# Smaller first x pieces kept on chip, a layer norm spread under gate tiles, and later rms statistics in an eight-core encoder block

## Chip, cores and metric

The kernel runs on all 8 cores of one Trainium2 chip. Each core takes half of one of four sequences (2048 tokens and a halo) and needs nothing from the others. The metric is device microseconds of the slowest core. A core has TensorE (PE, matmuls), VectorE (DVE), ScalarE (ACT), GpSimd (POOL), a sync engine (SP) that here only issues transfers, and 16 DMA engines. GpSimd also issues the transfers of the weights, which the program declares f32 in memory and bf16 on the core (the records show each as 128 packets of 2 KB). Matmuls write to PSUM, of which the program rotates six banks, one tile each.

## The reference, cut to what matters

```python
u = rms_norm(h, g_mix)                         # h: 16 meta tokens, then x
z = u @ w_in                                   # [value | gate | pool | gate A | gate B], 1024 each
y_conv = silu(layer_norm(dwconv31(value * sigmoid(gate)))) @ w_conv_out
y_pool = multi_scale_pool(pool) @ w_pool ... @ w_pool_out
h = h + (sigmoid(gateA) * y_conv + sigmoid(gateB) * y_pool) @ w_o
v = rms_norm(h, g_ffn)
h = h + (silu(v @ w_ffn_gate) * (v @ w_ffn_up)) @ w_ffn_down
out = rms_norm(h, g_final)
```

Activations lie with the 1024 channels on partitions (8 blocks of 128, index c or k) and tokens along the row. A "tile" below is one output block of 128 channels by up to 512 tokens, made by 8 accumulating matmuls. The stages on PE are: pool tiles (the head), value/gate tiles with the depthwise convolution, the layer norm with gate tiles A(c,b), B(c,b), pool products P(c,b) and conv products C(c,b) for channel block c and token block b, the output projection, the gate/up tiles of the channel mixer, and the down projection.

## The kernel before

Every operation goes through a small scheduler that derives semaphore waits from the memory touched, in granules of 64 bytes:

```python
GRAN = 64
def gran(self, ap):                  # cut
    lo = (base + o) // GRAN
    hi = (base + o + span - 1) // GRAN + 1
```

The head takes x in five pieces of 416 tokens. Pieces wait for weights on the sync queue:

```python
x_load(0)
for _ in range(2): load_one()        # pool weights 0 and 1
S.wait_prod(POOL, x_sem[0])
prefetch()                           # the other weights, as slots allow (9 slots)
S.wait_prod(SP, slot_sem[3]);  x_load(1)
S.wait_prod(SP, slot_sem[7]);  x_load(2);  x_load(3)
# per piece: squares on ACT, adder tree on DVE, one f32 ones matmul,
# Ln and Exp on ACT, eight scalings of x into uT (bf16) on DVE, eight pool tiles
```

After the convolution come eight f32 statistic matmuls, Ln and Exp, then the folding of two pool weights into one (`weff`), and 32 normalising steps on DVE that are handed out in the background (`pump`). In the output projection the row statistics work like this:

```python
def sumsq(src, n, c, eng, w_=TT):
    a = ac1[n % 2][:, 0:w_]
    if c == 0:
        act(a, src, AF.Square)
    else:
        q = sq1[c % 3][:, 0:w_]              # three scratch tiles in turn
        act(q, src, AF.Square)
        tt(eng, a, a, q, ALU.add)            # on GpSimd here

def rms_stat(n, w_=TT):
    mm(psum[6][:, 0:w_], ones[:], ac1[n % 2][:, 0:w_], True, True)
    t = sq1[0][:, 0:w_]                      # scratch tile 0 again
    act(t, psum[6][:, 0:w_], AF.Ln, bias=e_rms)
    act(psum[7][:, 0:w_], t, AF.Exp, scale=-0.5)

for b in range(NB):
    for c in range(KC):
        ...                                  # 8 matmuls into one of 6 PSUM banks
        tt(DVE, h, ps[:], h, ALU.add)        # residual add, frees the bank
        sumsq(h, b, c, POOL)
        if c == 2 and b > 0:
            rms_stat(b - 1)
            v_norm(b - 1)                    # eight DVE scalings, 5.4 us
```

Of the kernel before, what the change touches and what calls it, by code (L numbers as in the profile page):

```python
# [7 lines left out]
F32 = mybir.dt.float32  # L8
# [5 lines left out]
KC = 8  # L14
# [15 lines left out]
RMS_EPS = 1e-6  # L30
LN_EPS = 1e-5
NSLOT = 9
HW_ = TOK // 2
RW = HW_ + 28
RWP = 1056
# [155 lines left out]
def build_nc():  # L191
# [3 lines left out]
    def din(name, shape, dt=F32):  # L195
        return nc.dram_tensor(name, list(shape), dt, kind="ExternalInput")

    xp_d = din("xp", [NPC, 128, KC * PW])
    xr_d = din("xr", [NB, 128, KC * TT])
    w_in = din("w_in", [40, 128, 1024])  # L200
    w_co = din("w_conv_out", [8, 128, 1024])
# [50 lines left out]

    uT = at("uT", [128, KC, EXT], BF16, oA)
    psb = [at(f"psb{c}", [128, EXT], F32, oB + c * EXT * 4) for c in range(KC)]
    mT = at("mT", [128, KC, TOK], BF16, oM)
    slot = [at(f"wslot{i}", [128, 1024], BF16, oS + i * 2048) for i in range(NSLOT)]
    slotf = [at(f"wslotf{i}", [128, 512], F32, oS + i * 2048) for i in range(NSLOT)]
# [10 lines left out]
    weff = at("weff", [128, KC, 1024], BF16, oW)  # L268


    xoffs = [oM, oM + 13312, oZ, oW]
    xb = [at(f"xb{i}", [128, KC, PW], F32, o) for i, o in enumerate(xoffs)]
    sq0 = [at(f"sq0_{i}", [128, KC, PW], F32, oZ + 13312 * (1 + i)) for i in range(2)]
    lnt = at("lnt", [128, TT], F32, oZ + 13312 * 3)
    assert 13312 * 3 + 2048 <= NZT * 2048


    z = oZ
# [57 lines left out]
    def dsem(name):  # L336
        return Prod(sem(name))

    cst = dsem("d_const")
    slot_sem = [dsem(f"d_slot{i}") for i in range(NSLOT)]  # L340
    x_sem = [dsem(f"d_x{i}") for i in range(4)]
    rep_sem = [dsem(f"d_rep{i}") for i in range(2)]
    ad_sem = [dsem(f"d_ad{i}") for i in range(2)]
    h1_sem = [dsem(f"d_h1{i}") for i in range(3)]
# [38 lines left out]
    for c in range(KC):  # L383
        wl.append((f"val{c}", w_in.ap()[c], False))
        wl.append((f"gate{c}", w_in.ap()[8 + c], False))
    wl.append(("gA0", w_in.ap()[24], False))
    for g in range(4):
        wl.append((f"wpl{g}", w_pl.ap()[g], True))
        wl.append((f"po{2 * g}", w_po.ap()[2 * g], False))
        wl.append((f"po{2 * g + 1}", w_po.ap()[2 * g + 1], False))  # L390
    for c in range(KC):
        if c:
            wl.append((f"gA{c}", w_in.ap()[24 + c], False))
        wl.append((f"gB{c}", w_in.ap()[32 + c], False))
        if c != 0:
            wl.append((f"co{c - 1}", w_co.ap()[c - 1], False))
    wl.append(("co7", w_co.ap()[7], False))
    for c in range(KC):
        wl.append((f"wo{c}", w_o.ap()[c], False))
# [40 lines left out]
            bg.popleft()()  # L440


    for (o, i_) in ((pc[:], pc_d.ap()), (invc[:], ic_d.ap()), (emask[:], em_d.ap())):
        S.dma(SP, cst, o, i_, val=48)
    S.op(DVE, lambda e: e.memset(ones[:], 1.0 / D), [], [ones[:]])
    S.op(DVE, lambda e: e.memset(eps[:, 0:1], RMS_EPS), [], [eps[:, 0:1]])
    S.op(DVE, lambda e: e.memset(eps[:, 1:2], LN_EPS), [], [eps[:, 1:2]])
    e_rms, e_ln = eps[:, 0:1], eps[:, 1:2]
    for r_ in rep:
        S.gran(r_[:])  # L450


    def x_load(p):
        q = p % 4
        S.dma(SP, x_sem[q], xb[q][:].rearrange("p k t -> p (k t)"), xp_d.ap()[p])

    x_load(0)
    for _ in range(2):
        load_one()
    S.wait_prod(POOL, x_sem[0])  # L460
    prefetch()
    S.wait_prod(SP, slot_sem[3])
    x_load(1)
    S.wait_prod(SP, slot_sem[7])
    x_load(2)
    x_load(3)

    def s1_squares(p):
        x = xb[p % 4]
        sq = sq0[p % 2]  # L470
        for h in range(4):
            act(sq[:, 2 * h:2 * h + 2, :], x[:, 2 * h:2 * h + 2, :], AF.Square)
        tt(DVE, sq[:, 0:2, :], sq[:, 0:2, :], sq[:, 2:4, :], ALU.add)
        tt(DVE, sq[:, 4:6, :], sq[:, 4:6, :], sq[:, 6:8, :], ALU.add)
        tt(DVE, sq[:, 0:2, :], sq[:, 0:2, :], sq[:, 4:6, :], ALU.add)
        tt(DVE, sq[:, 0, :], sq[:, 0, :], sq[:, 1, :], ALU.add)

    def s1_rstd(p):
        mm(psum[6][:, 0:PW], ones[:], sq0[p % 2][:, 0, :], True, True)
        act(lnt[:, 0:PW], psum[6][:, 0:PW], AF.Ln, bias=e_rms)  # L480
        act(psum[7][:, 0:PW], lnt[:, 0:PW], AF.Exp, scale=-0.5)

    def s1_scale(p):
        x = xb[p % 4]
        for k in range(KC):
            stt(DVE, uT[:, k, p * PW:(p + 1) * PW], x[:, k, :], pcc(PC_GMIX, k), psum[7][:, 0:PW],
                ALU.mult, ALU.mult)

    def pool_tile(p, c):
        b = nb()  # L490
        for k in range(KC):
            mm(b[:, 0:PW], w(f"pool{c}", k), uT[:, k, p * PW:(p + 1) * PW], k == 0, k == KC - 1)
        act(psb[c][:, p * PW:(p + 1) * PW], b[:, 0:PW], AF.Copy)

    s1_squares(0)
    s1_rstd(0)
    s1_scale(0)
    for p in range(NPC):
        if p + 1 < NPC:
            s1_squares(p + 1)  # L500
        for c in range(KC):
            pool_tile(p, c)
            if c == 2 and p + 1 < NPC:
                s1_rstd(p + 1)
                s1_scale(p + 1)
            if p == NPC - 1:
                release(f"pool{c}")
        if p == 0:
            x_load(4)


    win_done = set()
# [141 lines left out]
    ln_done = set()  # L654

    def C(c, b):
        pump_until(ln_done, b)
        ps = tile_mm(f"co{c}", lambda k: actT[k][b][:])
        i, j = sA.pop((c, b)), t2.pop((c, b))
        tt(DVE, zt[i][:], ps[:], zt[i][:], ALU.mult)  # L660
        tt(DVE, mrg[c][b][:], zt[i][:], zt[j][:], ALU.add)
        zfree.append(i)
        zfree.append(j)
# [9 lines left out]
    pump(len(bg))  # L673

    lnm = {}
    for b in range(NB):
        tok = slice(b * TT, (b + 1) * TT)
        if b == NB - 1:
            pm, pq = psum[6], psum[7]
        else:  # L680
            pm, pq = nb(), nb()
        mm(pm[:], ones[:], acc_s[:, tok], True, True)
        mm(pq[:], ones[:], acc_q[:, tok], True, True)
        i = ztile()
        act(zt[i][:], pm[:], AF.Square)
        if b == NB - 1:
            mean, rstd = pm, psum[7]
            ids = (i,)
        else:
            m_ = ztile()  # L690
            act(zt[m_][:], pm[:], AF.Copy)
            mean, rstd = zt[m_], zt[i]
            ids = (i, m_)
        tt(DVE, zt[i][:], pq[:], zt[i][:], ALU.subtract)
        act(zt[i][:], zt[i][:], AF.Ln, bias=e_ln)
        act(rstd[:], zt[i][:], AF.Exp, scale=-0.5)
        lnm[b] = (mean, rstd, ids)

    def ln_steps(b):
        mean, rstd, ids = lnm[b]  # L700
        out = []
        for c in range(KC):
            def step(c=c):
                d = d_sb[c][b][:]
                tt(DVE, d, d, mean[:], ALU.subtract)
                tt(DVE, d, d, rstd[:], ALU.mult)
            out.append(step)

        def fin():
            for c in range(KC):  # L710
                act(actT[c][b][:], d_sb[c][b][:], AF.Silu, bias=pcc(PC_LNB, c), scale=pcc(PC_LNG, c))
            zfree.extend(ids)
            ln_done.add(b)
        last = out.pop()
        out.append(lambda: (last(), fin()))
        return out

    for b in range(NB):
        bg.extend(ln_steps(b))


    for g in range(4):
        s_ = whome[f"wpl{g}"]
        for km in range(2):
            src = slotf[s_][:, km * 256:(km + 1) * 256]
            ts(DVE, wps[:, g, km, :], src, pcc(PC_PSC, 2 * g + km), ALU.mult)
        for ki in range(2):
            for h in range(2):
                ps = nb()
                for km in range(2):  # L730
                    mm(ps[:], wps[:, g, km, ki * 128:(ki + 1) * 128],
                       w(f"po{2 * g + km}", None, h * 512, (h + 1) * 512), km == 0, km == 1)
                act(weff[:, 2 * g + ki, h * 512:(h + 1) * 512], ps[:], AF.Copy)
            pump(1)
        release(f"wpl{g}", f"po{2 * g}", f"po{2 * g + 1}")
    zfree.extend((0, 1))

    for b in range(NB):
        Bm(0, b)
        pump(1)  # L740
        P(0, b)
        pump(1)
    release("gB0")
    for c in range(1, KC):
        for b in range(NB):
            A(c, b)
            pump(1)
            Bm(c, b)
            pump(1)
            P(c, b)  # L750
            pump(1)
        release(f"gA{c}", f"gB{c}")
        for b in range(NB):
            C(c - 1, b)
        release(f"co{c - 1}")

    def x_res(b):
        q = b % 3
# [32 lines left out]
    for b in range(NB):  # L791
        for c in range(KC):
# [5 lines left out]
            sumsq(h, b, c, POOL)  # L798
            if b == NB - 1:
                release(f"wo{c}")  # L800
            if c == 2 and b > 0:
                rms_stat(b - 1)
                v_norm(b - 1)
                if b == 1:
                    x_res(3)
# [10 lines left out]
        act(s_, pg[:], AF.Silu)  # L816
        tt(DVE, fT[j][:, tok], pu[:], s_, ALU.mult)

    gu(0, 0)
    rms_stat(3)  # L820
    gu(0, 1)
    v_norm(3)
    gu(0, 2)
    for b in range(3):
        gu(1, b)
    gu(0, 3)
# [79 lines left out]
def _host_inputs(inputs):  # L906
# [37 lines left out]
    for core in range(NCORES):  # L944
# [8 lines left out]
        for g, w in enumerate(WINS):  # L953
# [7 lines left out]
                    cnt = min(t + right + 1, T) - max(t - left, 0)  # L961
                invc[:, g * 8 + jj] = 1.0 / cnt
        m = dict(shared)
        m["xp"] = np.ascontiguousarray(
            xe.reshape(NPC, PW, KC, 128).transpose(0, 3, 2, 1)).reshape(NPC, 128, KC * PW)
        m["xr"] = np.ascontiguousarray(
            xe[HALO:HALO + TOK].reshape(NB, TT, KC, 128).transpose(0, 3, 2, 1)).reshape(NB, 128, KC * TT)
        m["invc"] = invc
# [23 lines left out]
```

## Time and profile before

| | before |
|---|---|
| time, median of the runs | 1092.04 us |
| slowest profiled core | 1089.8 us |
| PE busy | 93% of the span |
| 128x512 tile, start to start | 1.73 us |

The page of the profile before: busy time by engine, and the chain of work that ended last, by engine.

```profile
PE 1009.8 (93%) x5628; PEld 485.2 (45%) x5628; DVE 455.7 (42%) x698; ACT 312.3 (29%) x495; POOL 128.8 (12%) x160
PE 84%; DVE 4%; DMA 4%; ACT 3%; issue 3%; POOL 2%; DVEq 0%; SPq 0%; ACTq 0%; POOLq 0%
```

PE is the engine to save time on, but "busy" hides how: a matmul at half clock is busy too. So the waits of PE are read by stretch. First the head (0 to 112 us), then the layer norm (285 to 372), then the output projection (535 to 625). Columns: who waited for whom, us in total, number of waits, longest.

```profile
PE ps L352 <- DVE sq_0_180 L366: 28.3, 3, 23.0
PE ps L352 <- DVE sq_1_181 L366: 9.2, 2, 6.6
PE ps L352 <- DVE uT L373: 2.5, 1, 2.5
...
PE ps L352 <- DVE wps L369: 6.2, 1, 6.2
PE ps L352 <- ACT act_3_128 L363: 4.5, 1, 4.5
PE ps L352 <- DMA wslot_66<-w_pool_out: 1.8, 1, 1.8
...
PE ps L352 <- POOL ac_1_224 L366: 9.1, 2, 5.1
PE ps L352 <- POOL ac_0_223 L366: 1.4, 1, 1.4
```

The first line holds the start: 23.0 of its 28.3 us pass before the first matmul, the rest are waits for squares of later pieces. In the layer norm PE waits for VectorE to get to the fold's input, and at the end for the activations of token block 3. In the projection it waits for GpSimd's sums. Elsewhere the profile shows one wait of PE, 2.0 us for the last row statistics (after 1060 us), which is why only these three places could give much time.

### The profile page before, as it was taken

Reading aid. Unit: us, or ns where it says so; the run is one execution under the profiler, and the core shown is the slowest. Engines: PE = TensorE matmul, PEld = TensorE weight load, DVE = VectorE, ACT = ScalarE, POOL = GpSimd, SP = SyncE. Lnnn points to the kernel's source line nnn. Section 1 sums busy time; section 2 is a strip of 40 time slices with the busy share of each in tenths; the row PEclk is TensorE's granted clock in tenths of the full one; section 3 lists DMA queues with packets and bytes.
Section 4 is the critical chain, followed back from the end, with each engine's and each line's share of the span. In section 5 each row is a group of like instructions: output and inputs, shape, how many; then the busy total and the mean of one; then the engine's idle time right before and its main releaser. Section 6 shows DMA issues by size and latency. Waiting matters only on the chain.

```text
span 1089.8 us, 15507 instructions; the slowest of 8 cores (1081.2 to 1089.8 us)
## 1 busy us (share of the span) xinstructions
PE 1009.8 (93%) x5628; PEld 485.2 (45%) x5628; DVE 455.7 (42%) x698; ACT 312.3 (29%) x495; POOL 128.8 (12%) x160
## 2 busy tenths in 40 slices
PE   0789999999879699999998799999999999999996
PEld 0344555555324244444443344444444444444485
DVE  1453679984358633322346332222112222233454
ACT  2354234333677512222133421111111111121121
POOL 1000212421020000000044501111000000000000
PEclk9899999999979899999999899999999999999998
DMA  7801797766461111111465734544322200603112
GB/s 138 269 1 19 134 184 153 169 146 145 92 104 31 21 29 29 30 29 30 115 233 193 177 56 74 91 89 88 65 39 35 35 1 2 230 1 155 78 78 78
DMA packets 34234, 99.90 MB, mean 92 GB/s; under 512 B 4080, under 2 KB 7280, under 8 KB 31600
## 3 DMA queue, kind: packets, MB, share of 16 engines
q0 software_dynamic: 17024, 35.13, 20.1%
q1 hardware_dynamic: 17136, 63.77, 19.8%
q8 instruction: 47, 0.77, 0.3%
q14 instruction: 27, 0.22, 0.1%
HBM read 111.93 MB, written 21.04 MB: 122 GB/s over the span
## 4 chain that ended last, share of the span: by engine, by line
PE 84%; DVE 4%; DMA 4%; ACT 3%; issue 3%; POOL 2%; DVEq 0%; SPq 0%; ACTq 0%; POOLq 0%
PE ps L352 79%; PE ps L594 5%; DMA xb_176<-xp 1%; DMA xb_177<-xp 1%; POOL ac_1_224 L366 1%; DMA wslot_62<-w_in 1%; DMA wslot_61<-w_pool_out 1%; DVE vT L373 1%; POOL ac_0_223 L366 1%; DVE sq_0_180 L366 0%; DVE sq_1_181 L366 0%; ACT sq_0_180 L363 0%; ACT sq_1_181 L363 0%; ACT L363 0%; ACT sq_0_220 L363 0%
## 5 line engine op out<-in xcount | busy, mean ns | idle before, releaser
L352 PE MATMUL ps<-mT,weff 128*128 128x512 bf16 x256 | 60.5, 379 | 0.0
L352 PE MATMUL ps<-uT,wslot_63 128*128 128x416 bf16 (+1 forms) x216 | 47.7, 365 | 0.0
L352 PE MATMUL ps<-uT,wslot_60 128*128 128x416 bf16 (+1 forms) x216 | 47.7, 365 | 0.0
L352 PE MATMUL ps<-uT,wslot_62 128*128 128x416 bf16 (+1 forms) x184 | 44.4, 390 | 0.0
L363 ACT ACTIVATE sgf_225<-ps 128x512 f32<-128x512 f32 x30 | 17.9, 598 | 82.6 <-PE ps L352 82.6
L363 ACT ACTIVATE sgf_227<-ps 128x512 f32<-128x512 f32 x29 | 17.3, 598 | 81.5 <-PE ps L352 81.5
L363 ACT ACTIVATE sgf_226<-ps 128x512 f32<-128x512 f32 x29 | 17.3, 598 | 80.2 <-PE ps L352 80.2
L352 PE MATMUL ps<-vT,wslot_62 128*128 128x512 bf16 x160 | 39.1, 388 | 0.0
L352 PE MATMUL ps<-uT,wslot_61 128*128 128x416 bf16 (+1 forms) x184 | 38.9, 354 | 0.0
L352 PEld LDWEIGHTS ps<-mT,weff 128*128 128x128 bf16 x256 | 25.1, 98 | 30.4 <-issue 0.3
L352 PE MATMUL ps<-uT,wslot_64 128*128 128x512 bf16 (+1 forms) x176 | 38.3, 363 | 0.0
L352 PE MATMUL ps<-vT,wslot_60 128*128 128x512 bf16 x160 | 37.8, 379 | 0.0
L352 PE MATMUL ps<-vT,wslot_61 128*128 128x512 bf16 x160 | 37.8, 379 | 0.0
L352 PE MATMUL ps<-vT,wslot_63 128*128 128x512 bf16 x160 | 37.8, 379 | 0.0
L352 PE MATMUL ps<-vT,wslot_64 128*128 128x512 bf16 x160 | 37.8, 379 | 0.0
L352 PE MATMUL ps<-vT,wslot_66 128*128 128x512 bf16 x160 | 37.8, 379 | 0.0
L352 PE MATMUL ps<-vT,wslot_67 128*128 128x512 bf16 x160 | 37.8, 379 | 0.0
L352 PE MATMUL ps<-vT,wslot_59 128*128 128x512 bf16 x160 | 37.8, 379 | 0.0
L352 PEld LDWEIGHTS ps<-uT,wslot_63 128*128 128x128 bf16 x216 | 21.6, 101 | 22.9 <-issue 3.4
L352 PEld LDWEIGHTS ps<-uT,wslot_60 128*128 128x128 bf16 x216 | 21.5, 100 | 21.4 <-issue 1.2
L352 PE MATMUL ps<-uT,wslot_66 128*128 128x416 bf16 (+1 forms) x144 | 30.9, 357 | 0.0
L352 PE MATMUL ps<-vT,wslot_65 128*128 128x512 bf16 x128 | 30.2, 379 | 0.0
(1655 smaller groups left out, 1952.4 us busy)
## 6 DMA issues: line engine op xcount, KB each, us to landing
rep_186<-ad SPq DMA_DIRECT2D x32, 263.0 KB, 6.5
rep_187<-ad SPq DMA_DIRECT2D x32, 263.0 KB, 8.0
h1b_217<-xr SPq DMA_DIRECT2D x2, 2048.0 KB, 10.7
h1d<-h1b_217 SPq DMA_DIRECT2D x2, 2048.0 KB, 8.0
h2b_259<-h1d SPq DMA_DIRECT2D x2, 2048.0 KB, 8.5
xb_176<-xp SPq DMA_DIRECT2D x2, 1664.0 KB, 15.1
h1b_218<-xr SPq DMA_DIRECT2D x1, 2048.0 KB, 19.1
h1b_219<-xr SPq DMA_DIRECT2D x1, 2048.0 KB, 11.5
```

What stands on the lines that cost most here:

```text
L352: S.op(PE, lambda e: e.matmul(out, lhsT=lhsT, rhs=rhs, start=start, stop=stop), [lhsT, rhs], [out], signal=stop if signal is None else signal)
L363: S.op(ACT, lambda e: e.activation(out=out, in_=in_, func=func, scale=scale, **kw), reads, [out])
L366: S.op(eng, lambda e: e.tensor_tensor(out=out, in0=a, in1=b, op=op), [a, b], [out])
L373: S.op(eng, lambda e: e.scalar_tensor_tensor(out=out, in0=a, scalar=s, in1=b, op0=op0, op1=op1), [a, b] + ([] if isinstance(s, float) else ...
L594: S.op(PE, lambda e, o=o, lt=lt, r_=r_, q=q, j=j: e.matmul(o, lhsT=lt, rhs=r_, start=(q == 0), stop=(q == 7), tile_position=(0, 32 * j)), ...
```

## The change

It has three parts. The head gets pieces of 160, 320 and four times 400 tokens that all have a place of their own, with piece 0's statistics summed on PE instead of in an adder tree. The layer norm's statistics go between A(1) tiles, the folds between B tiles, and the silu just ahead of its use. The rms statistics of the output projection move from tile 2 to tile 6 of the next block, and the last one behind three gate/up tiles.

```diff
+PIECES = ((0, 160), (160, 320), (480, 400), (880, 400), (1280, 400), (1680, 400))
...
+    x_load(0)
     for (o, i_) in ((pc[:], pc_d.ap()), (invc[:], ic_d.ap()), (emask[:], em_d.ap())):
         S.dma(SP, cst, o, i_, val=48)
+    for p in range(1, NX):
+        x_load(p)
+    load_one()
+    S.wait_prod(POOL, x_sem[0])
+    prefetch()
...
-    S.wait_prod(SP, slot_sem[3])
-    x_load(1)
-    S.wait_prod(SP, slot_sem[7])
-    x_load(2)
-    x_load(3)
...
+    def s1_norm(p):
+        ks = (0, 4, 1, 5, 2, 6, 3, 7) if p == 0 else (0,)
+        for i, k in enumerate(ks):
+            mm(st, ones[:], sqx[:, k, o:o + n], i == 0, i == len(ks) - 1)
...
+    for p in range(2, NX):
         for c in range(KC):
             pool_tile(p, c)
-            if c == 2 and p + 1 < NPC:
-                s1_rstd(p + 1)
-                s1_scale(p + 1)
+            if c == 2 and p + 1 < NX:
+                s1_norm(p + 1)
+            if c == 5 and p + 2 < NX:
+                s1_squares(p + 2)
...
+    for b in range(NB):
+        A(1, b)
+        ln_stat(b)
+    for b in range(NB):
+        ln_rstd(b)
+        bg.extend(ln_steps(b))
+    for b in range(NB):
+        Bm(0, b)
+        pump(1)
+    fold(0)
+    pump(2)
+    B1(0)
+    B1(1)
+    fold(1)
+    pump(2)
+    B1(2)
+    fold(2)
+    pump(2)
+    B1(3)
+    fold(3)
+    zfree.extend((0, 1))
...
-            if c == 2 and b > 0:
+            if c == 6 and b > 0:
                 rms_stat(b - 1)
                 v_norm(b - 1)
...
-    gu(0, 0)
+    for b in range(3):
+        gu(0, b)
     rms_stat(3)
-    gu(0, 1)
     v_norm(3)
-    gu(0, 2)
```

More of the change, by code (lines that the diff above doesn't have):

```diff
@@ L32 @@
 NSLOT = 9
+PIECES = ((0, 160), (160, 320), (480, 400), (880, 400), (1280, 400), (1680, 400))
+NX = len(PIECES)
 HW_ = TOK // 2
@@ L196, in din @@
         return nc.dram_tensor(name, list(shape), dt, kind="ExternalInput")
-    xp_d = din("xp", [NPC, 128, KC * PW])
+    xp_d = din("xp", [128, KC * EXT])
     xr_d = din("xr", [NB, 128, KC * TT])
@@ L254, in build_nc @@
     psb = [at(f"psb{c}", [128, EXT], F32, oB + c * EXT * 4) for c in range(KC)]
+    sqx = at("sqx", [128, KC, EXT], F32, oB)
     mT = at("mT", [128, KC, TOK], BF16, oM)
@@ L268, in build_nc @@
     weff = at("weff", [128, KC, 1024], BF16, oW)
-    xoffs = [oM, oM + 13312, oZ, oW]
-    xb = [at(f"xb{i}", [128, KC, PW], F32, o) for i, o in enumerate(xoffs)]
-    sq0 = [at(f"sq0_{i}", [128, KC, PW], F32, oZ + 13312 * (1 + i)) for i in range(2)]
-    lnt = at("lnt", [128, TT], F32, oZ + 13312 * 3)
-    assert 13312 * 3 + 2048 <= NZT * 2048
+    xoffs = [oM, oM + 160 * 32, oM + 480 * 32, oW, oZ, oZ + 400 * 32]
+    xb = [at(f"xb{i}", [128, KC, n], F32, o) for i, ((_, n), o) in enumerate(zip(PIECES, xoffs))]
     z = oZ
@@ L340, in build_nc @@
     slot_sem = [dsem(f"d_slot{i}") for i in range(NSLOT)]
-    x_sem = [dsem(f"d_x{i}") for i in range(4)]
+    x_sem = [dsem(f"d_x{i}") for i in range(NX)]
     rep_sem = [dsem(f"d_rep{i}") for i in range(2)]
@@ L385, in build_nc, with wl_gate, wl_po @@
         wl.append((f"gate{c}", w_in.ap()[8 + c], False))
-    wl.append(("gA0", w_in.ap()[24], False))
+    def wl_gate(n, c):
+        wl.append((f"g{n}{c}", w_in.ap()[(24 if n == "A" else 32) + c], False))
+    def wl_po(n):
+        wl.append((f"po{n}", w_po.ap()[n], False))
+    wl_gate("A", 0)
+    wl_gate("A", 1)
+    wl_gate("B", 0)
     for g in range(4):
         wl.append((f"wpl{g}", w_pl.ap()[g], True))
-        wl.append((f"po{2 * g}", w_po.ap()[2 * g], False))
-        wl.append((f"po{2 * g + 1}", w_po.ap()[2 * g + 1], False))
-    for c in range(KC):
-        if c:
-            wl.append((f"gA{c}", w_in.ap()[24 + c], False))
-        wl.append((f"gB{c}", w_in.ap()[32 + c], False))
-        if c != 0:
-            wl.append((f"co{c - 1}", w_co.ap()[c - 1], False))
+    wl_po(0)
+    wl_po(1)
+    wl_gate("B", 1)
+    for n in range(2, KC):
+        wl_po(n)
+    for c in range(2, KC):
+        wl_gate("A", c)
+        wl.append((f"co{c - 2}", w_co.ap()[c - 2], False))
+        wl_gate("B", c)
+    wl.append(("co6", w_co.ap()[6], False))
     wl.append(("co7", w_co.ap()[7], False))
@@ L440, in pump_until, with x_load @@
             bg.popleft()()
+    def x_load(p):
+        o, n = PIECES[p]
+        S.dma(SP, x_sem[p], xb[p][:].rearrange("p k t -> p (k t)"), xp_d.ap()[:, KC * o:KC * (o + n)])
+    x_load(0)
     for (o, i_) in ((pc[:], pc_d.ap()), (invc[:], ic_d.ap()), (emask[:], em_d.ap())):
         S.dma(SP, cst, o, i_, val=48)
+    for p in range(1, NX):
[3 more added lines that the diff above has]
+    prefetch()
     S.op(DVE, lambda e: e.memset(ones[:], 1.0 / D), [], [ones[:]])
@@ L448, in build_nc @@
     e_rms, e_ln = eps[:, 0:1], eps[:, 1:2]
-    for r_ in rep:
-        S.gran(r_[:])
-    def x_load(p):
-        q = p % 4
-        S.dma(SP, x_sem[q], xb[q][:].rearrange("p k t -> p (k t)"), xp_d.ap()[p])
-    x_load(0)
-    for _ in range(2):
-        load_one()
-    S.wait_prod(POOL, x_sem[0])
-    prefetch()
-    S.wait_prod(SP, slot_sem[3])
-    x_load(1)
-    S.wait_prod(SP, slot_sem[7])
-    x_load(2)
-    x_load(3)
-    def s1_squares(p):
-        x = xb[p % 4]
-        sq = sq0[p % 2]
+    act(tmp8[:, 0:1], e_rms, AF.Ln, bias=e_rms)
+    def s1_squares(p):
+        o, n = PIECES[p]
+        x = xb[p]
+        sq = sqx[:, :, o:o + n]
+        if p == 0:
+            for h in range(4):
+                act(sq[:, h, :], x[:, h, :], AF.Square)
+                tt(DVE, sq[:, 4 + h, :], x[:, 4 + h, :], x[:, 4 + h, :], ALU.mult)
+            return
         for h in range(4):
@@ L476, in s1_squares @@
         tt(DVE, sq[:, 0, :], sq[:, 0, :], sq[:, 1, :], ALU.add)
-    def s1_rstd(p):
-        mm(psum[6][:, 0:PW], ones[:], sq0[p % 2][:, 0, :], True, True)
-        act(lnt[:, 0:PW], psum[6][:, 0:PW], AF.Ln, bias=e_rms)
-        act(psum[7][:, 0:PW], lnt[:, 0:PW], AF.Exp, scale=-0.5)
-    def s1_scale(p):
-        x = xb[p % 4]
+    def s1_norm(p):
+        o, n = PIECES[p]
+        st = psum[6][:, 0:n]
+        ks = (0, 4, 1, 5, 2, 6, 3, 7) if p == 0 else (0,)
+        for i, k in enumerate(ks):
+            mm(st, ones[:], sqx[:, k, o:o + n], i == 0, i == len(ks) - 1)
+        act(st, st, AF.Ln, bias=e_rms)
+        act(psum[7][:, 0:n], st, AF.Exp, scale=-0.5)
         for k in range(KC):
-            stt(DVE, uT[:, k, p * PW:(p + 1) * PW], x[:, k, :], pcc(PC_GMIX, k), psum[7][:, 0:PW],
+            stt(DVE, uT[:, k, o:o + n], xb[p][:, k, :], pcc(PC_GMIX, k), psum[7][:, 0:n],
                 ALU.mult, ALU.mult)
     def pool_tile(p, c):
+        o, n = PIECES[p]
         b = nb()
         for k in range(KC):
-            mm(b[:, 0:PW], w(f"pool{c}", k), uT[:, k, p * PW:(p + 1) * PW], k == 0, k == KC - 1)
-        act(psb[c][:, p * PW:(p + 1) * PW], b[:, 0:PW], AF.Copy)
+            mm(b[:, 0:n], w(f"pool{c}", k), uT[:, k, o:o + n], k == 0, k == KC - 1)
+        act(psb[c][:, o:o + n], b[:, 0:n], AF.Copy)
+        if p == NX - 1:
+            release(f"pool{c}")
     s1_squares(0)
-    s1_rstd(0)
-    s1_scale(0)
-    for p in range(NPC):
-        if p + 1 < NPC:
-            s1_squares(p + 1)
+    s1_norm(0)
+    s1_squares(1)
+    for c in range(4):
+        pool_tile(0, c)
+    s1_norm(1)
+    s1_squares(2)
+    for c in range(4):
+        pool_tile(1, c)
+    for c in range(4, KC):
+        pool_tile(0, c)
+        pool_tile(1, c)
+        if c == 5:
+            s1_norm(2)
+        if c == 6:
+            s1_squares(3)
+    for p in range(2, NX):
         for c in range(KC):
             pool_tile(p, c)
-            if c == 2 and p + 1 < NPC:
-                s1_rstd(p + 1)
-                s1_scale(p + 1)
-            if p == NPC - 1:
-                release(f"pool{c}")
-        if p == 0:
-            x_load(4)
+            if c == 2 and p + 1 < NX:
+                s1_norm(p + 1)
+            if c == 5 and p + 2 < NX:
+                s1_squares(p + 2)
     win_done = set()
@@ L656, in C @@
     def C(c, b):
-        pump_until(ln_done, b)
         ps = tile_mm(f"co{c}", lambda k: actT[k][b][:])
@@ L675, in build_nc, with ln_stat @@
     lnm = {}
-    for b in range(NB):
+    def ln_stat(b):
         tok = slice(b * TT, (b + 1) * TT)
@@ L694, in build_nc, with ln_rstd @@
         tt(DVE, zt[i][:], pq[:], zt[i][:], ALU.subtract)
-        act(zt[i][:], zt[i][:], AF.Ln, bias=e_ln)
-        act(rstd[:], zt[i][:], AF.Exp, scale=-0.5)
         lnm[b] = (mean, rstd, ids)
+    def ln_rstd(b):
+        mean, rstd, ids = lnm[b]
+        act(zt[ids[0]][:], zt[ids[0]][:], AF.Ln, bias=e_ln)
+        act(rstd[:], zt[ids[0]][:], AF.Exp, scale=-0.5)
     def ln_steps(b):
@@ L707, in ln_steps, with silu, wps_scale @@
             out.append(step)
-        def fin():
-            for c in range(KC):
-                act(actT[c][b][:], d_sb[c][b][:], AF.Silu, bias=pcc(PC_LNB, c), scale=pcc(PC_LNG, c))
-            zfree.extend(ids)
-            ln_done.add(b)
         last = out.pop()
-        out.append(lambda: (last(), fin()))
+        out.append(lambda: (last(), zfree.extend(ids), ln_done.add(b)))
         return out
-    for b in range(NB):
-        bg.extend(ln_steps(b))
-    for g in range(4):
+    def silu(b):
+        pump_until(ln_done, b)
+        for c in range(KC):
+            act(actT[c][b][:], d_sb[c][b][:], AF.Silu, bias=pcc(PC_LNB, c), scale=pcc(PC_LNG, c))
+    def wps_scale(g):
         s_ = whome[f"wpl{g}"]
@@ L726, in build_nc, with fold @@
             ts(DVE, wps[:, g, km, :], src, pcc(PC_PSC, 2 * g + km), ALU.mult)
+    def fold(g):
         for ki in range(2):
@@ L733, in build_nc @@
                 act(weff[:, 2 * g + ki, h * 512:(h + 1) * 512], ps[:], AF.Copy)
-            pump(1)
         release(f"wpl{g}", f"po{2 * g}", f"po{2 * g + 1}")
-    zfree.extend((0, 1))
+    for g in range(4):
+        wps_scale(g)
+    for b in range(NB):
+        A(1, b)
+        ln_stat(b)
+    release("gA1")
+    for b in range(NB):
+        ln_rstd(b)
+        bg.extend(ln_steps(b))
     for b in range(NB):
@@ L740, in build_nc, with B1 @@
         pump(1)
-        P(0, b)
-        pump(1)
     release("gB0")
-    for c in range(1, KC):
+    def B1(b):
+        while not zfree:
+            pump(1)
+        Bm(1, b)
+        pump(2)
[7 more added lines that the diff above has]
+    fold(2)
+    pump(2)
+    B1(3)
+    release("gB1")
+    fold(3)
+    zfree.extend((0, 1))
+    for c in range(2):
+        for b in range(NB):
+            P(c, b)
+            pump(2)
+            if b == 1:
+                silu(c)
+    for c in range(2, KC):
         for b in range(NB):
             A(c, b)
-            pump(1)
+            pump(2)
+            C(c - 2, b)
             Bm(c, b)
-            pump(1)
+            pump(2)
+            if c == 2 and b < 2:
+                silu(b + 2)
             P(c, b)
-            pump(1)
-        release(f"gA{c}", f"gB{c}")
-        for b in range(NB):
-            C(c - 1, b)
-        release(f"co{c - 1}")
+        release(f"gA{c}", f"co{c - 2}", f"gB{c}")
+    for b in range(NB):
+        C(6, b)
+    release("co6")
     def x_res(b):
@@ L963, in _host_inputs @@
         m = dict(shared)
-        m["xp"] = np.ascontiguousarray(
-            xe.reshape(NPC, PW, KC, 128).transpose(0, 3, 2, 1)).reshape(NPC, 128, KC * PW)
+        m["xp"] = np.concatenate(
+            [xe[o:o + n].reshape(n, KC, 128).transpose(2, 1, 0).reshape(128, KC * n) for o, n in PIECES], 1)
         m["xr"] = np.ascontiguousarray(
```

## The prediction

> **What bounds the kernel now.** TensorE (PE): the chain of waits puts 84% of the 1089.8 us span on it. A 128x512 tile of 8 matmuls takes 1.73 us start to start, a 128x416 one 1.41 (timeline). In 112-285, 372-560 and 625-1060 us PE waits for nothing (waits). The losses:
>
> 1. Head, 0-112 us. The first pool matmul starts at 27.3: x piece 0 (1.7 MB) lands at 15.3, then table load 1.3, squares and adds 6.3, ones matmul 1.7, Ln and Exp 1.3. From there to 112.1 PE needs 40 tiles x 1.41 + 4 x 0.8 = 60 us and takes 85: waits of 6.6 and three of 2.6 us for squares.
> 2. Layer norm, 290-371.4: 24 tiles, 6.9 us of statistics and 6.9 of fold need 55 us, taken 81.5. Loss 26: the first fold waits 6.2, C(0,3) 4.5 + 3 x 0.8 for activations, w_pool_out 3.
> 3. Output projection, 565-620: 43 us of PE work in 55. PE waits 10.5 us for GpSimd sums, because each v_norm (5.4 us of VectorE) holds up the residual adds before a statistic is due.
>
> **What the change does.**
>
> Head: piece 0 is 0.66 MB, first in its queue (estimate: lands near 6 us); eight f32 ones matmuls replace the adder tree. First pool matmul near 13.5 us, 14 earlier. But x loads no longer wait for weights. In 28-34 us of the trace both queues moved about 19 packets per us each, one for one (x 13 KB, weights 2 KB)[...]. So pool weights 1 to 5 trail in 6.5 us apart (estimate: 13, 20, 27, 33, 39 us; the last two by 43), before four by 24. PE starves between 16 and 45. Also the kernel's dependency tracker works in 64-byte granules: the bf16 boundaries at columns 880 and 1680 fall inside one, so tiles (2,3) and (4,3) wait for the next piece's scaling, about 5 us each (Ln, Exp 1.4, eight scalings at 0.56). Pool stage ends near 101, not 112: gain 11 (5 to 18).
>
> Layer norm: A(1) tiles cover the statistics; folds and B tiles cover Ln/Exp and VectorE's 32 steps of 1.4 us (45 us, now the stage's floor). New stall: B(1,2) needs a buffer that only layer-norm block 1 frees, near 329, so ScalarE and then fold 3 wait 5-7 us. Loss falls from 26 to 12: gain 14 (8 to 18).
>
> Output projection: statistics at tile 6 instead of 2 give GpSimd time (1.44 us per add against 1.73 per tile); the last goes behind three gate/up tiles. Gain 10 of 12 (6 to 12).
>
> All is on PE's critical path.
>
> **Time:** 1092 - 35 = 1057 us, range 1046 to 1069. Faster by over 2% 0.93, within 2% 0.06, slower 0.01.
>
> **What would show each step.** Head: first pool matmul at 12-16 us; tiles (0,2) to (0,5) released by weight DMAs; waits of about 5 us on the uT scaling at (2,3) and (4,3); first conv-gate matmul at 95-107. Layer norm: no wait before the first fold, several us at fold 3 with ScalarE waiting for VectorE; stage about 14 shorter. Output projection: no PE wait for GpSimd over 2 us.
>
> **What would make it wrong.** Weights landing sooner than one packet per x packet; granule waits hidden behind others; longer half clock in a starved head.

The sum: 35 us, from 11 for the head, 14 for the layer norm and 10 for the projection. The packets stand by the trace before: from 28 to 34 us 102 weight packets and 111 of x start on core 3. So does the estimate of 6 us for x piece 0: there 1.7 MB took 12.9 us from issue to landing, so 0.66 MB takes about 5, issued at 1 us. Of the half clock, named as a risk, the same core had 6.8, 3.4 and 3.4 us in its head, from 41.3, 75.4 and 92.5 us.

## More of the kernel before

Cores 0 to 3 are the first die, 4 to 7 the second; the granted clock is the share of TensorE's full clock that a core got (0.973 to 0.978 in the profiled run before).

From 620 to 625 us on core 3 PE was busy 4.47 of 5.00 us with 9 matmuls at a mean clock of 0.51, in the 5 us after that 5.00 us with 25 at 1.00.

## The result, and the profile after

The kernel after takes 1076.22 us (median; fast runs 1075.74 to 1076.43) against 1092.04. The ratio of the fast runs is 0.9856, with a 95% interval of 0.9834 to 0.9879. Ratios here are the mean time of one kernel's fast runs over that of the other's of the same rounds, so not quite the ratio of the medians quoted. The gain is 15.8 us where 35 were predicted, and 1076 lies outside the predicted range. One of the four runs was slow (1252.69 us, one die at a granted clock of 0.81 to 0.82), and so was one of the kernel before (1113.88 us, counted in its median); the ratio leaves both out.

To see which stage gave what, I took from every core's trace the start of the first conv gate matmul, the last convolution matmul, the first matmul of the output projection and the first of the down projection. (The first of these is reckoned as the first convolution matmul less 28.34 us, the 160 matmuls ahead of it; read directly on one core of each it is 112.12 and 115.53 us.) Medians over the eight cores of the profiled runs, in us:

| stage | before | after | gained | predicted |
|---|---|---|---|---|
| start to first pool matmul | 26.9 | 13.1 | 13.8 | 14 |
| start to first conv gate matmul (the whole head) | 110.5 | 114.2 | -3.7 | 11 |
| value/gate tiles and convolution | 176.5 | 177.0 | -0.5 | 0 |
| end of the convolution to the output projection | 254.9 | 239.4 | 15.5 | 14 |
| output projection and gate/up | 377.3 | 375.6 | 1.7 | 10 |
| down projection to the end | 165.8 | 165.4 | 0.4 | 0 |
| span | 1086.0 | 1071.7 | 14.3 | 35 |

(Medians of stages do not add up exactly to the median span.) The layer norm did what was expected. Two stages did not. The head starts 13.8 us earlier and ends 3.7 us later, and the projection gave 1.7 us instead of 10.

The page after, the same two lines:

```profile
PE 1014.0 (94%) x5708; PEld 493.1 (46%) x5708; DVE 456.2 (43%) x710; ACT 310.1 (29%) x509; POOL 128.7 (12%) x160
PE 83%; DVE 6%; DMA 5%; issue 2%; ACT 1%; POOL 1%; SPq 0%; DVEq 0%; ACTq 0%; POOLq 0%
```

PE's busy share says nothing of what happened: it rose by one point while a stage got longer. The waits of PE after (core 2), for the same three places (0 to 116, 285 to 372, 535 to 616 us):

```profile
PE ps L353 <- DVE uT L374: 10.1, 13, 2.4
PE ps L353 <- DVE sqx L367: 7.9, 2, 7.4
PE ps L353 <- DMA wslot_61<-w_in: 5.4, 1, 5.4
PE ps L353 <- DMA wslot_62<-w_in: 5.1, 1, 5.1
PE ps L353 <- DMA wslot_63<-w_in: 4.6, 1, 4.6
...
PE ps L353 <- ACT zt_203 L364: 4.8, 1, 4.8
PE ps L618 <- ACT dsq_193 L364: 1.6, 1, 1.6
...
PE ps L353 <- DVE h1b_219 L367: 4.1, 1, 4.1
PE ps L353 <- DMA wslot_64<-w_ffn_up: 1.5, 1, 1.5
PE ps L353 <- DVE h1b_218 L367: 0.9, 1, 0.9
```

All but 0.5 us of the waits for later pieces' squares are gone (the 7.4 us left in `sqx` is the start, before the first matmul), and so are the fold's wait for `wps` and the waits for GpSimd. In the head there are new ones for weights (three of about 5 us) and for `uT`, the scaled input, 13 times instead of once. In the layer norm the fold waits 4.8 us for a B tile's sigmoid to free its bank (`zt`). In the projection there is a new wait for `h1b`, a residual add that had not yet freed its PSUM bank.

The matmuls of the head after, in order of time (start, us, count at the end, and in brackets the wait just before and its releaser):

```profile
13.46 2.33 PE L353 MATMUL ps<-uT,wslot_60 128*128 128x160 bf16 x8 [1.48 <-DVE uT L374]
21.16 1.22 PE L353 MATMUL ps<-uT,wslot_61 128*128 128x160 bf16 x8 [5.36 <-DMA wslot_61<-w_in]
27.50 1.23 PE L353 MATMUL ps<-uT,wslot_62 128*128 128x160 bf16 x8 [5.12 <-DMA wslot_62<-w_in]
33.35 1.23 PE L353 MATMUL ps<-uT,wslot_63 128*128 128x160 bf16 x8 [4.62 <-DMA wslot_63<-w_in]
34.37 1.35 PE L353 MATMUL ps<-sqx,ones_s 128*128 128x320 f32 x2
...
59.24 0.91 PE L353 MATMUL ps<-sqx,ones_s 128*128 128x400 f32 x2 [0.54 <-DVE sqx L367]
62.57 0.77 PE L353 MATMUL ps<-uT,wslot_63 128*128 128x400 bf16 x2 [2.42 <-DVE uT L374]
63.55 0.33 PE L353 MATMUL ps<-uT,wslot_63 128*128 128x400 bf16 x1 [0.21 <-DVE uT L374]
66.54 2.87 PE L353 MATMUL ps<-uT,wslot_64 128*128 128x400 bf16 x8
69.21 2.33 PE L353 MATMUL ps<-uT,wslot_65 128*128 128x400 bf16 x8
71.38 1.52 PE L353 MATMUL ps<-uT,wslot_66 128*128 128x400 bf16 x8
```

Two things are to be seen. After the first tile PE does one tile of piece 0 per weight, at 21.16, 27.50 and 33.35 us, and idles between them. And after piece 3's statistic at 59.24 the next pool tile, which is one of piece 2, waits for the scaling of piece 3, matmul by matmul, until 66.5 us; the two tiles after it take 2.67 and 2.17 us start to start where the next takes 1.35. They run at half clock: the trace of this core (core 2) gives the clock as 0.5 from 64.0 to 70.9 us. By stretch (us, PE busy and count, then the mean granted clock):

```profile
66.50:71.40 4.90, 4.90 (x18) 0.55 0.01 3
```

The same happens from 90.7 to 102 us with piece 5.

### The profile page after: what moved, and what is told of

It reads as the page before. It is cut to its first block, busy times and chain, and to the rows that moved or that the text cites. A ratio compares the mean times of both kernels' runs of the same rounds, so it can differ in the third digit from the quotient of the medians.

```text
span 1073.3 us, 15749 instructions; the slowest of 8 cores (1070.5 to 1074.0 us)
## 1 busy us (share of the span) xinstructions
PE 1014.0 (94%) x5708; PEld 493.1 (46%) x5708; DVE 456.2 (43%) x710; ACT 310.1 (29%) x509; POOL 128.7 (12%) x160
## 4 chain that ended last, share of the span: by engine, by line
PE 83%; DVE 6%; DMA 5%; issue 2%; ACT 1%; POOL 1%; SPq 0%; DVEq 0%; ACTq 0%; POOLq 0%
PE ps L353 79%; PE ps L618 5%; DMA wslot_63<-w_in 2%; DVE vT L374 1%; DMA rep_186<-ad 1%; DMA rep_187<-ad 1%; DMA ad<-aT_183 1%; POOL ac_0_223 L367 1%; POOL ac_1_224 L367 0%; DVE uT L374 0%; DMA xb_177<-xp 0%; ACT ps L364 0%; DVE sqx L367 0%; DVE h2b_259 L374 0%; SPq L190 0%
## 5 line engine op out<-in xcount | busy, mean ns | idle before, releaser
L353 PE MATMUL ps<-uT,wslot_60 128*128 128x512 bf16 (+4 forms) x224 | 51.1, 357 | 4.5 <-DVE uT L374 4.3
L353 PE MATMUL ps<-uT,wslot_65 128*128 128x512 bf16 (+4 forms) x216 | 47.1, 366 | 0.0
L353 PE MATMUL ps<-uT,wslot_61 128*128 128x416 bf16 (+4 forms) x192 | 40.5, 357 | 4.4 <-DMA wslot_61<-w_in 4.4
L353 PE MATMUL ps<-uT,wslot_62 128*128 128x416 bf16 (+4 forms) x192 | 39.5, 350 | 5.1 <-DMA wslot_62<-w_in 5.1
L353 PE MATMUL ps<-uT,wslot_64 128*128 128x416 bf16 (+4 forms) x192 | 41.5, 363 | 0.9 <-DVE zt_200 L367 0.9
L353 PE MATMUL ps<-vT,wslot_67 128*128 128x512 bf16 x160 | 39.3, 381 | 1.6 <-DVE vT L374 1.4
L353 PE MATMUL ps<-uT,wslot_63 128*128 128x416 bf16 (+3 forms) x128 | 28.0, 346 | 12.1 <-DMA wslot_63<-w_in 5.8
L353 PE MATMUL ps<-vT,wslot_64 128*128 128x512 bf16 x160 | 38.8, 386 | 0.0
L353 PE MATMUL ps<-vT,wslot_63 128*128 128x512 bf16 x160 | 37.8, 379 | 0.0
L353 PE MATMUL ps<-vT,wslot_66 128*128 128x512 bf16 x160 | 37.8, 379 | 0.0
L353 PE MATMUL ps<-vT,wslot_61 128*128 128x512 bf16 x160 | 37.8, 379 | 0.0
L353 PE MATMUL ps<-vT,wslot_62 128*128 128x512 bf16 x160 | 37.8, 379 | 0.0
L353 PE MATMUL ps<-vT,wslot_68 128*128 128x512 bf16 x160 | 37.8, 379 | 0.0
L353 PE MATMUL ps<-vT,wslot_65 128*128 128x512 bf16 x160 | 37.8, 379 | 0.0
L353 PE MATMUL ps<-uT,wslot_68 128*128 128x416 bf16 (+1 forms) x144 | 30.9, 357 | 0.0
```

What stands on the lines that cost most here:

```text
L353: S.op(PE, lambda e: e.matmul(out, lhsT=lhsT, rhs=rhs, start=start, stop=stop), [lhsT, rhs], [out], signal=stop if signal is None else signal)
```

## The experiments

Twelve runs. The first four ran on a chip whose second die showed a slightly lower granted clock in most runs (in the profiled run of experiment 3 its cores had 0.959 to 0.975, those of the first die 0.976 to 0.984); there I read the cores of the first die, and two of the four were repeated elsewhere. The control first.

**The kernel after, again** (no edit).

> The kernel after, unchanged, as a control on the chip of these runs: 0.985 of before, cores of an undisturbed die near 1072 us.

Measured: 1076.61 us, 0.9857 of before (0.9840 to 0.9873). The stages repeat the table: head 114.1, layer norm 239.5, projection and gate/up 375.6 us. One run was slow.

**1. Is the head part a loss?** The head of the kernel before, with the new layer norm and rms parts (the diff is the head's part of the change, undone).

> The new layer norm and rms parts with the head of the kernel before (five pieces of 416, weights first, adder tree). Theory D (the head part lost 3.7 us, the layer norm gained 15.8, the projection 2): 1071 to 1074 us, 2 to 5 us faster than the kernel after. Rival, the prediction's reading (head gains about 11, the miss lies elsewhere): slower than after by 8 us or more, 1084 or above.

Measured: first-die medians of 1067.7 to 1068.9 us in the fast runs, against 1071.3 to 1073.5 for the kernel after on its chips; 0.9835 of before (0.9802 to 0.9869); head 111.3 us. As a whole the fast runs took 1075.4 to 1080.0 us, more than expected, since the second die lagged by 1.1 to 6.2 us (medians), and the ratio alone does not tell this kernel from the kernel after. By the first die and the stage the head part costs about 3 to 4 us. The prediction's reading, that the head gained and something else lost (1084 us or more), falls.

**2. Granule waits.** The same pieces cut at multiples of 32 columns, so that no bf16 boundary falls inside a 64-byte granule:

```diff
-PIECES = ((0, 160), (160, 320), (480, 400), (880, 400), (1280, 400), (1680, 400))
+PIECES = ((0, 160), (160, 320), (480, 416), (896, 384), (1280, 416), (1696, 384))
```

> Kernel after, with the x pieces cut at columns that are multiples of 32 (896 and 1696 in place of 880 and 1680), so that no bf16 piece boundary shares a 64-byte granule of the dependency tracker. Theory A (granule stalls): tiles (2,3) and (4,3) stop waiting for the next piece's scaling; each such wait costs 5.0 us plus 2.1 to 2.3 us of half-clock tiles after it, so the time falls by 12 to 15 us, to about 1062, and the conv stage starts near 101 us instead of 115 (core 2). Rival (ScalarE and VectorE do not keep up with squares and scaling): the waits stay, within 2 us of 1076.

> Aligned pieces again, now beside the other runs of this call, since in its first run one die was held at a lower clock: 1061 to 1064 us on both dies, 0.972 to 0.975 of before.

Measured: the first run gave first-die medians of 1059.8 and 1060.8 us in its two fast runs, with the other die slower (1065.8 and 1065.1 us; in the profiled one its cores had a granted clock of 0.965 to 0.970 against 0.973 to 0.977; 0.9764 of before as a whole); the second, on another chip, 1064.58 us, 0.9750 of before (0.9726 to 0.9774). The head ends at 101.7 us in both instead of 114.1. PE's matmuls on core 1 of the second run, around the same statistic (start, us):

```profile
60.20 0.88 PE L353 MATMUL ps<-sqx,ones_s 128*128 128x384 f32 x2 [0.31 <-DVE sqx L367]
60.92 3.33 PE L353 MATMUL ps<-uT,wslot 128*128 128x416 bf16 x18
```

The statistic is followed at once by pool matmuls. Both waits are gone, and so are the half-clock stretches after them (6.8 us each on core 2 of the kernel after, from 64.0 and 94.8 us; here the clock was 1.0 in the trace from 45 us on through the head, and the 18 matmuls from 60.92 us take 0.18 us each). The 12.4 us saved in the median head are their price. From the first tile of piece 2 to the end of the head, the cores of the kernel after and of its control took 60.4 to 62.6 us, and all cores of both runs here 47.9: 12.5 to 14.7 us less, 6 to 7 for each wait with the half clock after it. The rival, that ScalarE and VectorE could not keep up, falls: they do the same work here.

**3. Weights behind x packets.** Piece 2 waits for pool weight 3, pieces 3 to 5 for weight 6:

```diff
-    for p in range(1, NX):
-        x_load(p)
+    x_load(1)
     load_one()
     S.wait_prod(POOL, x_sem[0])
     prefetch()
+    S.wait_prod(SP, slot_sem[3])
+    x_load(2)
+    S.wait_prod(SP, slot_sem[6])
+    for p in range(3, NX):
+        x_load(p)
```

> Kernel after, with x pieces 2 to 5 held back on the sync queue: piece 2 until pool weight 3 has landed, pieces 3 to 5 until weight 6 has. Theory B (one weight packet per x packet starves PE): weight 3 lands by about 20 us instead of 33, PE reaches piece 2 near 40 us instead of 52.8, gain 8 to 13 us. Rival (the sum of bytes is the limit, order does not matter): piece 2 starts no earlier or later pieces of x come late by as much, time within 2 us of 1076.

Measured (chip with the slower second die): first-die medians of 1059.6 to 1060.6 us, head 102.3 us, 11.8 less than the control; 0.9786 of before (0.9758 to 0.9814). The first tiles now follow closely, on core 0:

```profile
13.83 2.33 PE L353 MATMUL ps<-uT,wslot 128*128 128x160 bf16 x8 [1.48 <-DVE uT L374]
16.36 1.22 PE L353 MATMUL ps<-uT,wslot 128*128 128x160 bf16 x8 [0.20 <-DMA wslot<-w_in]
18.06 2.52 PE L353 MATMUL ps<-uT,wslot 128*128 128x160 bf16 x16 [0.48 <-DMA wslot<-w_in]
20.71 1.40 PE L353 MATMUL ps<-sqx,ones_s 128*128 128x320 f32 x2
```

The same bytes are moved, so it was the order, not the amount. That leaves open why weights came so late. From piece 2 on the head takes as long as before (median 61.7 us), so this loss is apart from that of experiment 2.

**4. Is it one weight packet per x packet?** Nothing is held back, but each x piece from 1 on is loaded as two transfers of half a row:

```diff
-        S.dma(SP, x_sem[p], xb[p][:].rearrange("p k t -> p (k t)"), xp_d.ap()[:, KC * o:KC * (o + n)])
+        hs = ((0, 4), (4, 8)) if p else ((0, 8),)
+        tot = 16 * len(hs)
+        for lo, hi in hs:
+            S.dma(SP, x_sem[p], xb[p][:, lo:hi, :].rearrange("p k t -> p (k t)"),
+                  xp_d.ap()[:, KC * o + lo * n:KC * o + hi * n], val=tot)
```

> Kernel after, with each of the x pieces 1 to 5 loaded as two transfers of half the row (6.4 KB packets in place of 12.8), same bytes, same order, no added wait. Theory B (one weight packet per x packet): weights get twice the share, about 4 us apart in place of 6.4, weight 3 in by 23 to 26 us instead of 33, piece 2 reached 4 to 8 us earlier, gain 3 to 8 us. Rival (weights are late for another reason, such as the issue or the sum of bytes): weight 3 at 33 us still, no gain.

Measured: 1070.44 us, 0.9799 of before (0.9785 to 0.9814); head 107.7 us, 6.4 less than the control. PE on core 1:

```profile
13.92 2.27 PE L353 MATMUL ps<-uT,wslot 128*128 128x160 bf16 x8 [1.48 <-DVE uT L374]
19.13 1.23 PE L353 MATMUL ps<-uT,wslot 128*128 128x160 bf16 x8 [2.94 <-DMA wslot<-w_in]
22.86 1.22 PE L353 MATMUL ps<-uT,wslot 128*128 128x160 bf16 x8 [2.50 <-DMA wslot<-w_in]
26.88 1.23 PE L353 MATMUL ps<-uT,wslot 128*128 128x160 bf16 x8 [2.80 <-DMA wslot<-w_in]
```

The weights come 3.7 to 4.0 us apart instead of 5.9 to 6.3. The DMA records of the kernel after (core 2), counted by their start:

```
us        x packets      weight packets (2 KB)
10-12     54             0
14-16     39             41
20-22     40             42
28-30     36             38
40-42     4              160
```

While x streams, as many packets of weights start as of x, about 20 a us of each. With half rows it is again one for one, at a higher rate (measured on core 1 of experiment 4: 62 weight rows and 64 x rows start from 16 to 18 us). The records do not name the DMA engine, so the order on one engine is not seen. A weight has 128 packets, so by estimate it takes 6.4 us at this rate and 1.6 at that of the last row, when x is nearly done; weights 1 to 3 took 6.3 to 7.1 us from first packet to last. The first row shows the second effect, which I had not foreseen: the first packet of weight 1 came 4.2 to 4.8 us after the start of the instruction that issued it (0.5 us long), over the eight cores, while rows of x were already queued. In the kernel before, with nothing queued, it was 1.2 to 2.4 us for weight 2. With half rows it was measured at 4.3 to 4.8 us, so halving them did not shorten it; its cause stays open.

**5. What the third part is worth.** Statistics again at tile 2, and the last behind one gate/up tile.

> Kernel after with the third part undone: rms statistics again at tile 2, the last one again behind one gate/up tile. Theory C: the third part as it stands swapped GpSimd waits for scratch waits and is worth about 2 us, so this takes 1077 to 1080 us. The prediction's reading (third part worth 10 us): 1084 to 1088.

Measured: 1079.55 us, 0.9888 of before (0.9865 to 0.9911). Projection and gate/up take 377.6 us instead of 375.6. The part as it stands is worth 2 us, not 10. The waits for GpSimd are back (core 2, 515 to 640 us), in place of those for `h1b`:

```profile
PE ps L353 <- POOL ac L367: 9.9, 3, 5.0
```

**6. The scratch tile.** The Ln of the statistic is written in place in PSUM, in two runs:

```diff
-        t = sq1[0][:, 0:w_]
+        t = psum[6][:, 0:w_]
```

> Kernel after, with the Ln of the rms statistics written in place in PSUM instead of into the scratch tile that the square of tile 6 also uses. Theory C (scratch collision): with the statistic at tile 6 the Ln waits until GpSimd has added tile 6's square (3.6 to 4.8 us of ScalarE idle, up to 7.9 us after the statistic), so VectorE scales late, residual adds of tile 7 wait behind it, and PE runs out of PSUM banks (0.9 and 4.1 us, half clock after). In place: Ln within 0.5 us of the statistic, those waits gone, also the 1.4 us on vT; gain 5 to 9 us. Rival (GpSimd's sums or VectorE's 5.4 us of scaling are the limit whatever the scratch): waits stay, within 2 us.

> Ln in place again, for the same reason: 1065 to 1068 us, 0.976 to 0.978 of before, within 3 us of the run with the other scratch tile (1070).

and, in a third, in the scratch tile that square 4 last used:

```diff
-        t = sq1[0][:, 0:w_]
+        t = sq1[1][:, 0:w_]
```

> Kernel after, with the Ln of the rms statistics in scratch tile 1 (last used by the square of tile 4) instead of tile 0 (used by that of tile 6). Theory C says that only the collision matters, not where the Ln is written: same gain as in place, 8 to 10 us on die 0. Rival (PSUM in place is what made it faster, by a shorter Ln): gain under 2 us.

Measured: the first run in place was as a whole 0.9854 (0.9810 to 0.9898), because the second die ran 6 to 11 us behind the first even in the fast runs; the first-die medians of these were 1063.0 to 1065.3 us. Repeated, 1069.56 us, 0.9796 (0.9761 to 0.9831), a little more than the 1065 to 1068 expected. The other scratch tile: 1069.95 us, 0.9798 (0.9784 to 0.9813). Projection and gate/up: 367.2 and 367.0 us, 8.4 to 8.6 less than the control. ScalarE in the kernel after (core 2), then in place (core 1), then with the other scratch tile (core 0), around the same statistic. The lines are the last square, the Ln and, in the first, the Exp:

```profile
578.63 0.63 ACT L364 ACTIVATE sq_0_220<-h1b_219 128x512 f32<-128x512 f32 x1 [0.78 <-POOL ac_0_223 L367]
582.88 0.69 ACT L364 ACTIVATE sq_0_220<-ps,eps_s 128x512 f32<-128x512 f32 x1 [3.61 <-POOL ac_0_223 L367]
583.65 0.60 ACT L364 ACTIVATE ps<-sq_0_220 128x512 f32<-128x512 f32 x1
```

```profile
575.89 0.63 ACT L364 ACTIVATE sq<-h1b 128x512 f32<-128x512 f32 x1 [0.78 <-POOL ac L367]
576.43 0.65 ACT L364 ACTIVATE ps<-ps,eps_s 128x512 f32<-128x512 f32 x1
```

```profile
573.53 0.63 ACT L364 ACTIVATE sq<-h1b 128x512 f32<-128x512 f32 x1 [0.78 <-POOL ac L367]
574.94 0.69 ACT L364 ACTIVATE sq<-ps,eps_s 128x512 f32<-128x512 f32 x1 [0.79 <-POOL ac L367]
```

In the kernel after, ScalarE has nothing to do for 3.61 us before the Ln and is released by a GpSimd sum. PE had made the statistic at 574.98, 7.9 us before. The Ln writes scratch tile 0, which holds the square of tile 6 (6 mod 3 is 0) until GpSimd adds it, and GpSimd is late. With the statistic at tile 2 the last user of scratch tile 0 was tile 6 of the block before, long done. The two mends agree to 0.2 us in the stage, so it is the collision and not PSUM that mattered. Contrary to what was expected of the run in place, the Ln did not come within 0.5 us of the statistic: on core 1 of the repeated run it began 3.8 us after it (572.66 and 576.43), because on ScalarE it comes behind squares that themselves wait for GpSimd. What it held up (VectorE, kernel after, core 2):

```profile
575.25 0.69 DVE L367 TENSOR_TENSOR h1b_219<-ps,h1b_219 128x512 f32<-128x512 f32 x1 [0.28 <-PE ps L353]
584.36 5.36 DVE L374 SCALAR_TENSOR_TENSOR vT<-h1b_218,pc_s,ps 128x512 bf16<-128x512 f32 x8 [8.42 <-ACT ps L364]
589.63 0.68 DVE L367 TENSOR_TENSOR h1b_219<-ps,h1b_219 128x512 f32<-128x512 f32 x1
```

VectorE idles 8.42 us for the Exp, scales for 5.36 us, and only then does the residual add of tile 7 that PE's bank waits for. PE waits 4.10 us for its bank, and the clock is 0.5 for 3.4 us from 589.7 us; after the 0.9 us wait at 571 us it stays at 1.00. In the repeated run in place PE has no such wait on any core; with the other scratch tile 0.9 to 1.1 us of it is left.

**7. All together.** Experiments 2, 3 and 6 in one kernel.

> Aligned pieces, weights first and Ln in place together. If the three causes are separate stretches of PE's time, the savings seen on die 0 one by one (12.6, 12.0 and 8.7 us against 1072) add up, less some overlap in the head: 1038 to 1043 us on an undisturbed die, 0.955 to 0.960 of before. Rival (the next limit takes over, for instance the x pieces themselves or fixed DMA time): at most the best two, 1050 or more.

Measured: 1043.05 us, 0.9551 of before (0.9537 to 0.9565); head 89.4, projection and gate/up 365.3 us. In the head 24.7 us are saved, 12.4 and 11.8 alone: the two causes act in different stretches and add up.

**8. The layer norm's own new wait.** On top of that, folds 1 to 3 come before B(1,2) and B(1,3), which then take the two buffers that the folds free, and fewer steps are pumped ahead of the P products:

```diff
     fold(0)
-    pump(2)
     B1(0)
-    B1(1)
     fold(1)
-    pump(2)
-    B1(2)
+    B1(1)
     fold(2)
-    pump(2)
-    B1(3)
-    release("gB1")
     fold(3)
     zfree.extend((0, 1))
+    B1(2)
+    B1(3)
+    release("gB1")
     for c in range(2):
         for b in range(NB):
             P(c, b)
-            pump(2)
+            pump(1)
...
-            if c == 2 and b < 2:
-                silu(b + 2)
+            if c == 2 and b == 0:
+                silu(2)
             P(c, b)
+            if c == 2 and b == 1:
+                silu(3)
```

> All three mends together, and the layer norm reordered: folds 1 to 3 before B(1,2) and B(1,3), which then take the two buffers the folds free instead of waiting for layer-norm block 1, and fewer normalising steps ahead of the P products (one per tile instead of two). Theory: in the kernel after the stage from the convolution's end to the output projection takes 239.4 us against 228 of PE work; the waits of 4.8, 1.0, 0.9 and 1.5 us go, gain 5 to 9 us, 1034 to 1038 us. Rival (VectorE's 45 us of steps set the stage whatever the order): under 2 us.

PE's waits between 260 and 372 us, in experiment 7 (core 1), then in this one (core 1):

```profile
PE ps L353 <- ACT zt L364: 5.9, 2, 4.8
PE ps L353 <- DVE zt L367: 1.5, 1, 1.5
```

```profile
PE ps L353 <- ACT zt L364: 1.7, 2, 1.0
PE ps L353 <- DMA wslot<-w_pool_out: 1.4, 2, 1.1
```

Measured: 1037.29 us, 0.9505 of before (0.9469 to 0.9542). The stage takes 233.4 instead of 239.5 us. The buffer wait is gone; small waits for the fold's weights come in its place. The result was right in every run. The two edits, order and pumping, were not tried apart, and experiment 7 ran on another chip than this one. This is the fastest version tried, 56 us under before and 39 under the kernel after by the medians.

## Why the prediction was wrong

*What bounds the kernel, and where the losses lie*: right. Only the three named places changed by more than 0.5 us.

*"First pool matmul near 13.5 us"*: right, 13.1.

*"Pool weights 1 to 5 trail in 6.5 us apart (estimate: 13, 20, 27, 33, 39 us; the last two by 43) ... PE starves between 16 and 45"*: weights did start one packet per x packet (42 and 40 from 20 to 22 us), and the term was mis-sized. The spacing was right (5.9 to 6.3 us between the first three tiles that waited, experiment 4 halving the packet and bringing it to about 4). The start was not: PE could use weight 1 at 21.2 us, not 13. On core 2 it was issued at 7.3 us, its first packet came at 12.1, its last at 19.0, and its landing was told at 21.0. The estimate fits x piece 0's landing (estimated 6 us, measured 6.7) plus one spacing (6.5 us); it has no room for the 4.8 us to the first packet nor for the 2.0 us from the last packet to the landing. PE reached piece 2 at 52.8 us, not 45. That is about 8 us of the miss. The order of loads costs 11.8 us in all (experiment 3).

*"Tiles (2,3) and (4,3) wait for the next piece's scaling, about 5 us each"*: right in place and cause (experiment 2), too small in size, because 6.8 us at half clock followed (core 2, from 64.0 and 94.8 us). I had named the half clock as a risk and left it out of the sum. From piece 2 to the end of the head the sum had 56 us (45 to 101) and the trace of core 2 has 62.7. With aligned pieces it is 47.9, so there each wait cost about 7.4 us, which is 4.8 of the 6.7 us of difference; 1.7 more is the first tile of piece 2, paced by the scaling at 0.54 us per matmul (3.03 us start to start instead of 1.35). With the 8 us above, this makes the head's 14.5 us.

*"Loss falls from 26 to 12: gain 14"* for the layer norm, with a new wait at B(1,2): right. The gain was 15.5 us, the longest new wait 4.8 us for that buffer, and experiment 8 got 6 us from it and its like.

*"Statistics at tile 6 instead of 2 give GpSimd time ... Gain 10 of 12"*: this step failed. PE's waits for GpSimd did go, as said, and yet the stage gave 1.7 us. I had checked GpSimd's rate and VectorE's order, not which scratch tile the Ln writes. At tile 6 it is the one that GpSimd still has to read. Without this collision the stage gives 377.3 - 367.2 = 10.1 us, the predicted 10 (experiment 6). So the reasoning about the bottleneck was sound and a storage hazard ate it.

The sum: 35 predicted; about 14.5 lost in the head and 8 in the projection, 1.5 won in the layer norm.

## What to carry to other kernels

Moving a step to another place in a loop also moves it against the rotation of its scratch buffers and against the alignment of its dependency tracker: list who last wrote and who still reads each buffer at the new place before counting on the gain. Count packets of two queues, not only bytes: in this trace as many weight packets of 2 KB started as x packets of 12.8 KB (42 and 40 in 2 us), the weights came 5.9 to 6.3 us apart, and holding back the x that was not needed yet was worth 11.8 us. And after a wait of PE read the clock in the trace: here 6.8 us at half clock followed waits of at most 2.42 us (core 2), and the forecast had no term for it.

## What the traces show besides

- Clock. On core 2 of the kernel after it fell to 0.5 at 64.0 us, though no wait of PE in the 20 us before was longer than 2.42 us; in the 3.4 us up to then PE was busy for 1.1 us. What makes it fall is not shown. Of the 119 stretches at 0.5 on the eight cores of the two profiles, 90 lasted 3.4 or 6.8 us; the longest, 27.3 and 30.7 us, lie in the starved head of five cores of the kernel after.
- States. In fast runs a core's mean granted clock was 0.95 to 1.00. Means of 0.81 to 0.85 on a whole die occur only in slow runs: 0.809 to 0.823 in the one of 1252.69 us and 0.823 to 0.852 in that of 1234.18 us, both of the kernel after. Why a die is slow is not shown.
- Table load of ScalarE. It took 1.28 us. On core 2 of the kernel after it began at 308.18 us, 0.02 us after the last activation's end, and the Ln began at 309.47, 0.01 us after it, so this switch cost about 1.3 us.
